# adaLN in the attention stages: from accumulations on VectorE to matrix products in quarters of TensorE's columns

## The chip, the cores and the metric

One core of one Trainium2 chip. The metric is the device time of one execution in microseconds (us), the median of several runs. TensorE (PE) multiplies; VectorE (DVE) and ScalarE (ACT) work elementwise; GpSimd (POOL) does little here; SyncE (SP) issues most of the DMA.

## What is computed

Two transformer blocks over 256 tokens of width 1024, in float32: a first block (gated recurrences, a long convolution, 32 experts of which each token uses two), then a second block of two layers (attention by retention and by a gated recurrence, then an MLP of width 4096). Every stage is modulated by adaLN: from a vector `c` come six vectors of 1024 (shift, scale and gate, twice), which are products of silu(c) with a 1024x6144 matrix.

```
def adaln(cvec, w, b):
    m = silu(cvec) @ w + b
    return split(m, 6)
...
mod_x = silu(c) @ ada_w[layer] + ada_b[layer]
mod_c = silu(c_ctx) @ ada_w[layer] + ada_b[layer]
...
hx = rmsnorm(x) * (1 + sc1) + sh1
```

In the second block's first layer both `c` and `c_ctx` need their vectors (two per matrix), in its second layer only `c` (one).

## The kernel before, in words

The kernel is written with a tile framework: the program's text gives instructions and priorities, and a scheduler decides at build time in which order each engine gets them, by its own estimate of times. Each engine then works through its list strictly in that order.

**Large products.** A weight tile of 1 MB is loaded into one of three `raw` buffers (`K.raw`, L175), split by ACT into a rounded part `whi` (L215) and by DVE into the rest `wlo` (L216), and multiplied in three products (`mm3`, L226 to L228). Their sums stand in PSUM: three buffers of the kind `mm`, two `tr`, three `at`.

**adaLN in two ways.** One adaLN vector set of 1024 columns is made in two **halves** of 512 columns, and a half needs two raw tiles of 512 x 512.
- `ada` (on DVE): for each of the 8 blocks of 128 rows and each vector, DVE scales the block by the vector's value in that row and adds it to `acc` (L287, L289). Then PE sums `acc` over the partitions, with one matrix product per 128 columns and vector that has a one in a single column (L296: 8 of them with two vectors, 4 with one), DVE copies (L299), PE transposes (L301), DVE copies (L302).
- `ada_pe` (on PE): 8 products per half with the two vectors as weights, 2 columns wide (L261), into an `mm` buffer; ACT copies the 2 rows (L265), PE transposes four times (L268).

A float32 product is two records in the trace, a transposition one.

**Where they run.** `ada_pe` makes one set at the program's start, one in the first block (`pieces`) and one ahead of the experts, from tiles that are already in memory (`adaw`). All others are `ada`: one at the start (two vectors), four in the first block (one vector), and in the second block three sets beside attention (gate, shift, scale; L1486) and one (layer 1) or three (layer 0) beside the MLP. They are generators in a list `s.bg`; `s.tick()` (called after a weight tile's load was written) runs one on to its next `yield`, which in `ada` comes after each raw tile.

**Attention** (block2). First the gated recurrence with four heads, one after the other, each a chain over all engines: PE transposes decayed keys (L1599), multiplies (L1613), DVE steps the state (L1628) and masks scores (L1637), PE makes the output (L1640, L1643). Beside it PE has the values `vr` (`values`, L1518 copies them from PSUM on ACT). Then retention, gates, output products.

Of the kernel before, what the change touches and what calls it, by code (L numbers as in the profile page):

```python
# [9 lines left out]
F32 = mybir.dt.float32  # L10
# [7 lines left out]
P = 128  # L18
# [8 lines left out]
def _consts():  # L27

    if CONSTS:
        return CONSTS  # L30
    f32, f64 = np.float32, np.float64
    p = np.arange(P)

    CONSTS["k_res"] = np.concatenate(
        [np.eye(P), np.tile((np.arange(24) == 15)[None], (P, 1)), np.tile(np.arange(8)[None], (P, 1))], 1).astype(f32)

# [86 lines left out]
class K:  # L123


    def __init__(self, nc, tc, I, out, cap=64, dbg=None):
# [12 lines left out]
        nc_ = nc  # L139
        self.kres = self.cp.tile([P, 160], F32, name="kres")  # L140
        nc_.scalar.dma_start(self.kres, I["k_res"])
        self.ident = self.kres[:, 0:128]
        self.hot = self.kres[:, 128:160]
        self.ones = self.cp.tile([P, 256], F32, name="ones")
# [100 lines left out]

    def ada_pe(self, pool, w, col0, s16, fin, got=()):

        nc = self.nc
        sv = s16.rearrange("p (i k) -> p k i", i=2)
        m = pool.tile([P, 16], F32, tag="adam", name="adam")  # L250
        for c in range(2):
            pt = self.mm()
            for q in range(2):
                if got:
                    v = got[c][:, 4 * q:4 * q + 4]
                else:
                    v = self.raw(w[512 * q:512 * q + 512, col0 + 512 * c:col0 + 512 * c + 512]
                                 .rearrange("(k p) c -> p k c", p=P))
                for kk in range(4):
                    k = 4 * q + kk  # L260
# [8 lines left out]
            nc.vector.tensor_copy(m.rearrange("p (i j) -> p j i", i=2)[:, 4 * c:4 * c + 4], p2[:, :, :2])  # L269
            yield  # L270
        fin(m)

    def ada(self, pool, w, col0, svecs, fin, tag="acc", src=()):
# [4 lines left out]
        for c in range(2):  # L278
            acc = pool.tile([P, nv, 512], F32, tag=tag, name="acc")
            for q in range(2):  # L280
# [10 lines left out]
                if q == 0:  # L291
                    yield
            n = 4 * nv
# [8 lines left out]
            nc.vector.tensor_copy(m.rearrange("p (i j) -> p i j", i=2)[:, :nv, 4 * c:4 * c + 4],  # L302
                                  p2[:, :n].rearrange("p (i j) -> p i j", j=4))
            if c == 1:
# [95 lines left out]
def params_c(s, pool):  # L400
# [7 lines left out]
    s.sc = s.cp.tile([P, 16], F32, name="sc")  # L408
    nc.scalar.activation(s.sc, pt[:, :16], AF.Silu)


# [15 lines left out]
def params(s, pool):  # L427
# [9 lines left out]
    s.sc2 = s.cp.tile([P, 16], F32, name="sc2")  # L437
    nc.scalar.activation(s.sc2, p1[:, 76:92], AF.Silu)
    s.cvw = p1[:, 0:36]
    s.n1g2 = [p1[:, 36 + 8 * l:44 + 8 * l] for l in range(2)]  # L440
# [92 lines left out]
def block1_mixer(s):  # L533
    nc, tc, I = s.nc, s.tc, s.I
    mt = nc.tensor.matmul
    with tc.tile_pool(name="p1", bufs=1) as pool_:
        pool = Pool(pool_, {"b8": 5, "b4": 3, "s4": 4, "t2": 6, "sq": 3,
                            "etot": 2, "adam": 2},
                    {"rstd": "s4", "nt": "sq", "prow": "sqo", "adarow": "sqo"})
        w_in = I["w_in"][0].rearrange("(k p) c -> p k c", p=P)  # L540
# [20 lines left out]

        both = [s.ada(pool, ada, 0, [sx, s.sc[:, 8:16]], fin0, "s4", (s.wp, "wlo")), s.ada_pe(pool, ada, 1024, s.sc, fin1)]
        for i in range(5):
# [79 lines left out]
        s.bg = [s.ada(pool, ada, 1024 * (i + 2), [sx], f) for i, f in enumerate((fin2, fin3, fin4, fin5))]  # L643
        pieces = s.ada_pe(pool, I["ada_w_2"][0], 0, s.sc2, fin0)

# [359 lines left out]
def moe(s):  # L1005
# [3 lines left out]
    with tc.tile_pool(name="pm", bufs=1) as pool_:  # L1009
        pool = Pool(pool_, {"xg": 2, "raw": 3, "sel": 2, "selT": 3, "hT": 2, "ws": 3, "glo": 3, "sq": 4},  # L1010
                    {"nt": "sq", "adarow2": "glo"})

        bias = s.adab2[0]

        def fin1(m):
            s.md2 += [fin_scale(s, m, 8 * i, bias[:, 8:16], s.n1g2[0], f"mA{i}") for i in range(2)]

        pieces = s.ada_pe(pool, I["ada_w_2"][0], 1024, s.sc2, fin1, s.adaw)
# [3 lines left out]
        tri, io64, io8 = km[:, 0:128], km[:, 128:256], s.kres[:, 152:160]  # L1022
        L = pool.tile([P, 2, 36], F32, name="L")
# [374 lines left out]
def block2(s):  # L1398
    nc, tc, I = s.nc, s.tc, s.I
    mt = nc.tensor.matmul  # L1400
    with tc.tile_pool(name="pb", bufs=1) as pool_:
        pool = Pool(pool_, {"b8": 5, "t2": 12, "nt": 3, "sx": 2, "rm": 1, "etot": 2, "st": 4},
                    {"sq": "t2", "acc": "b8"})
        kb = pool.tile([P, 2692], F32, name="kb2")
# [32 lines left out]
        def gla_params(l):  # L1437
# [9 lines left out]
            return gng, upst, gb  # L1447

        am = [pool.tile([P, 4, P], F32, name=f"am{i}") for i in range(2)]
        for a in am:  # L1450
            nc.gpsimd.memset(a, 0.0)

        for l in range(2):
# [508 lines left out]
```

## Time and profile before

| | us |
|---|---|
| three runs: median (lowest to highest) | 2025.29 (2024.18 to 2029.1) |
| the profiled execution | 2025.5 |
| its span in the trace | 2023.6 |
| TensorE busy in it | 1939.0 |
| VectorE busy | 1136.5 |
| ScalarE busy | 693.4 |

The span is the stretch from the first to the last instruction. PE's busy time counts overlapping records once; products overlap, and their ends are modelled, so that what one costs is read from the distance of starts. The stages: first block to 397 us, experts to about 890 us, second block's layer 0 with attention up to 1175 us and MLP up to 1540 us, layer 1 with attention up to 1790 us, then its MLP.

### The profile page before, as it was taken

Reading aid. Unit: us, or ns where it says so; the run is one execution under the profiler, and the core shown is the slowest. Engines: PE = TensorE matmul, PEld = TensorE weight load, DVE = VectorE, ACT = ScalarE, POOL = GpSimd, SP = SyncE. Lnnn points to the kernel's source line nnn. Section 1 sums busy time; section 2 is a strip of 40 time slices with the busy share of each in tenths; the row PEclk is TensorE's granted clock in tenths of the full one; section 3 lists DMA queues with packets and bytes.
Section 4 is the critical chain, followed back from the end, with each engine's and each line's share of the span. In section 5 each row is a group of like instructions: output and inputs, shape, how many; then the busy total and the mean of one; then the engine's idle time right before and its main releaser. Section 6 shows DMA issues by size and latency. Waiting matters only on the chain.

```text
span 2023.6 us, 27872 instructions
## 1 busy us (share of the span) xinstructions
PE 1939.0 (96%) x11492; PEld 1443.5 (71%) x11492; DVE 1136.5 (56%) x2110; ACT 693.4 (34%) x1023; POOL 32.2 (2%) x110
## 2 busy tenths in 40 slices
PE   6998989999999999989899999999999989999998
PEld 2866779844444444357678989778788967989998
DVE  5768795521101111144879959655634677887555
ACT  2564544421111111144432334131323454443444
POOL 0000000000000000000200000000000010000000
PEclk9999999999999999989989999999999989999999
DMA  8536546889999999953133424444423143457553
GB/s 285 167 105 208 167 130 231 309 364 421 421 421 421 420 421 421 421 205 104 43 125 126 149 82 135 157 146 135 135 84 104 56 148 114 156 197 229 175 180 104
DMA packets 218073, 426.15 MB, mean 211 GB/s; under 512 B 16427, under 2 KB 152584, under 8 KB 193112
## 3 DMA queue, kind: packets, MB, share of 16 engines
q1 hardware_dynamic: 208616, 419.75, 57.2%
q10 hardware_dynamic: 9200, 4.51, 0.8%
q8 instruction: 92, 1.51, 0.3%
q14 instruction: 37, 0.30, 0.0%
q0 software_dynamic: 128, 0.08, 0.0%
HBM read 423.26 MB, written 1.05 MB: 210 GB/s over the span
## 4 chain that ended last, share of the span: by engine, by line
PE 67%; DVE 6%; DMA 3%; ACT 2%; issue 1%; DVEq 0%; ACTq 0%; SPq 0%
PE mm L226 14%; PE mm L227 14%; PE mm L228 14%; PE mm L1271 10%; PE mm L1301 3%; PE at L1301 3%; DMA raw<-in_moe_w_down_dram 2%; PE at L1234 2%; PE at L1319 1%; PE tr L296 1%; DMA raw<-in_moe_w_up_dram 1%; DVE wlo L216 1%; DVE sx L1628 1%; DVE acc L289 1%; PE at L1712 1%
## 5 line engine op out<-in xcount | busy, mean ns | idle before, releaser
L228 PE MATMUL mm<-hh,wlo 128*128 128x256 f32 (+2 forms) x1232 | 406.3, 330 | 8.6 <-DVE wlo L216 8.6
L226 PE MATMUL mm<-hh,whi 128*128 128x256 f32 (+2 forms) x1232 | 411.4, 335 | 2.5 <-ACT hh L220 1.2
L227 PE MATMUL mm<-hl,whi 128*128 128x256 f32 (+2 forms) x1232 | 408.2, 332 | 0.1
L216 DVE TENSOR_TENSOR wlo<-raw,whi 128x2048 fp32r<-128x2048 f32 (+2 forms) x138 | 303.7, 2201 | 169.9 <-ACT whi L215 169.8
L215 ACT CAST whi<-raw 128x2048 fp32r<-128x2048 f32 (+2 forms) x138 | 253.1, 1834 | 354.0 <-PE mm L227 301.5
L228 PEld LDWEIGHTS mm<-hh,wlo 128*128 128x128 f32 (+1 forms) x1232 | 236.0, 192 | 33.3 <-DVE wlo L216 9.9
L226 PEld LDWEIGHTS mm<-hh,whi 128*128 128x128 f32 (+1 forms) x1232 | 236.2, 192 | 29.9 <-issue 3.8
L227 PEld LDWEIGHTS mm<-hl,whi 128*128 128x128 f32 (+1 forms) x1232 | 236.2, 192 | 25.7 <-issue 5.2
L289 DVE SCALAR_TENSOR_TENSOR acc<-raw,sc,acc 128x512 f32<-128x512 f32 x308 | 218.8, 746 | 13.9 <-DMA raw<-in_ada_w_dram 12.5
L226 PE MATMUL mm<-hidh,whi 128*128 128x256 f32 (+1 forms) x544 | 178.7, 331 | 0.0
L228 PE MATMUL mm<-hidh,wlo 128*128 128x256 f32 (+1 forms) x544 | 177.6, 330 | 0.1
L227 PE MATMUL mm<-hidl,whi 128*128 128x256 f32 (+1 forms) x544 | 177.3, 328 | 0.0
L1271 PE MATMUL mm<-raw,xg 128*64 128x512 f32 x736 | 172.5, 595 | 1.2 <-DMA raw<-in_moe_w_up_dram 1.2
L226 PE MATMUL mm<-whi,hh 128*128 128x256 f32 x512 | 150.1, 294 | 5.6 <-ACT vr L1518 3.6
L227 PE MATMUL mm<-wlo,hh 128*128 128x256 f32 x512 | 147.9, 289 | 3.0 <-DVE wlo L216 3.0
L228 PE MATMUL mm<-whi,hl 128*128 128x256 f32 x512 | 149.2, 292 | 0.7 <-DVE hl L371 0.7
L1271 PEld LDWEIGHTS mm<-raw,xg 128*64 128x64 f32 x736 | 54.6, 137 | 97.9 <-issue 93.2
L1279 DVE SCALAR_TENSOR_TENSOR glo<-mm,ws,glo 128x512 f32<-128x512 f32 x16 | 12.0, 751 | 191.1 <-PE mm L1271 169.2
L227 PEld LDWEIGHTS mm<-hidl,whi 128*128 128x128 f32 x544 | 102.3, 188 | 10.8 <-DVE hidl L221 0.6
L226 PEld LDWEIGHTS mm<-hidh,whi 128*128 128x128 f32 x544 | 101.9, 188 | 10.8 <-ACT hidh L220 0.7
L228 PEld LDWEIGHTS mm<-hidh,wlo 128*128 128x128 f32 x544 | 101.6, 188 | 11.0 <-DVE wlo L216 0.7
L226 PEld LDWEIGHTS mm<-whi,hh 128*128 128x128 f32 x512 | 99.6, 195 | 10.4 <-ACT vr L1518 4.8
(509 smaller groups left out, 2744.5 us busy)
## 6 DMA issues: line engine op xcount, KB each, us to landing
raw<-in_ada_w_dram SPq DMA_DIRECT2D x68, 1024.0 KB, 5.2
raw<-in_w_mlp_dram SPq DMA_DIRECT2D x64, 1024.0 KB, 5.4
raw<-in_w_in_dram SPq DMA_DIRECT2D x48, 1024.0 KB, 5.2
raw<-in_moe_w_down_dram SPq DMA_DIRECT2D x48, 1024.0 KB, 16.8
raw<-in_moe_w_gate_dram SPq DMA_DIRECT2D x46, 1024.0 KB, 13.9
raw<-in_moe_w_up_dram SPq DMA_DIRECT2D x46, 1024.0 KB, 15.6
rawh<-in_moe_w_gate_dram SPq DMA_DIRECT2D x18, 1024.0 KB, 13.2
rawh<-in_moe_w_up_dram SPq DMA_DIRECT2D x18, 1024.0 KB, 12.6
```

Of the source, the lines that this page charges most:

```text
L215: self.nc.scalar.copy(hv, v)
L216: self.nc.vector.tensor_tensor(lv, v, hv, op=OP.subtract)
L226: mt(out, ah, bh, start=first, stop=False)
L227: mt(out, ah, bl, start=False, stop=False)
L228: mt(out, al, bh, start=False, stop=last)
L289: nc.vector.scalar_tensor_tensor(acc[:, i], v[:, kk], s[:, k:k + 1], acc[:, i], op0=OP.mult, op1=OP.add)
L296: nc.tensor.matmul(pt[:n, :P], self.hot[:, 15 - r:15 - r + n], acc[:, r // 4, (r % 4) * P:(r % 4 + 1) * P], start=r == 0, stop=r == n - 1)
L1234: mt(px, tk[:, a, k * P:(k + 1) * P], sel[:, a], start=tk is th and a == 0, stop=tk is tl and a == 1)
L1271: mt(pg[64 * j:64 * j + 64], xg[:, k, 2 * i + j], vs[j][:, kk], start=k == 0, stop=k == 7)
L1301: mt(pd[c][sl], hT[:, k, sl], vs[j][:, kk, 512 * c:512 * c + 512], start=k == 0, stop=k == 3)
L1319: mt(po[:, j], y[:, i, sl], selT[:, i], start=y is yh and i == 0, stop=y is yl and i == 1)
L1628: nc.vector.scalar_tensor_tensor(sxs[ps_, b_], sxs[ps_, a_], etot[ps_, a_:a_ + 1], adds[a_][ps_], op0=OP.mult, op1=OP.add)
```

## The change

- `ada_pe` now has weights of 32 columns: the two vectors and 30 columns of zeros (`sw`, `sw2`). The four products of a raw tile go to four quarters of PE's columns and so to four groups of 32 PSUM rows, instead of one after the other into the same two rows. The copy takes 128 rows (L267 of the new file), and four products with a 0/1 matrix `pick2` add up the quarters and turn the result (L270).
- `ada` does the same with its partial sums: the products for the four 128-column pieces go to the four quarters (L300), and one product with `pick8` takes the place of the transposition (L305).
- The three sets beside attention in each of the two layers go from `ada` to `ada_pe`, with `rest=False`: there is one `yield` per half, so one tick asks for two raw tiles.
- In the second block the buffers of `nt` (3) and the copies `adarow`, `adarow2` go into the pool `t2`, which has 13 instead of 12; in the first block `adarow2` goes into `t2` with 6.

```diff
+    def ada_pe(self, pool, w, col0, s32, fin, got=(), rest=True):
...
-                    nc.tensor.matmul(pt[:2], sv[:, k], v[:, kk], start=k == 0, stop=k == 7)
-                if q == 0:
+                    nc.tensor.matmul(pt[32 * kk:32 * kk + 32], s32[:, 4 * q + kk], v[:, kk], start=q == 0, stop=q == 1)
+                if q == 0 and rest:
                     yield
-            row = pool.tile([2, 512], F32, name="adarow2")
-            nc.scalar.copy(row, pt[:2])
+            row = pool.tile([P, 512], F32, tag="adarow2", name="adarow2")
+            nc.scalar.copy(row, pt)
             p2 = self.tr((P, 4, 128))
             for j in range(4):
-                nc.tensor.transpose(p2[:, j, :2], row[:, j * P:(j + 1) * P], self.ident[:2, :2])
+                nc.tensor.matmul(p2[:, j, :2], row[:, j * P:(j + 1) * P], self.pick2, start=True, stop=True)
...
     def ada(self, pool, w, col0, svecs, fin, tag="acc", src=()):
...
-            for r in range(n):
-                nc.tensor.matmul(pt[:n, :P], self.hot[:, 15 - r:15 - r + n],
-                                 acc[:, r // 4, (r % 4) * P:(r % 4 + 1) * P], start=r == 0, stop=r == n - 1)
-            row = pool.tile([8, P], F32, tag="adarow", name="adarow")
-            nc.vector.tensor_copy(row[:n], pt[:n, :P])
+            for i in range(nv):
+                for j in range(4):
+                    nc.tensor.matmul(pt[32 * j:32 * j + 32, :P], self.hot[:, 31 - i:63 - i],
+                                     acc[:, i, j * P:(j + 1) * P], start=i == 0, stop=i == nv - 1)
+            row = pool.tile([P, P], F32, tag="adarow", name="adarow")
+            nc.vector.tensor_copy(row, pt[:, :P])
             p2 = self.tr()
-            nc.tensor.transpose(p2[:, :n], row[:n], self.ident[:n, :n])
+            nc.tensor.matmul(p2[:, :4 * nv], row, self.pick8[:, :4 * nv], start=True, stop=True)
...
-        pool = Pool(pool_, {"b8": 5, "t2": 12, "nt": 3, "sx": 2, "rm": 1, "etot": 2, "st": 4},
-                    {"sq": "t2", "acc": "b8"})
+        pool = Pool(pool_, {"b8": 5, "t2": 13, "sx": 2, "rm": 1, "etot": 2, "st": 4},
+                    {"sq": "t2", "acc": "b8", "nt": "t2", "adarow": "t2", "adarow2": "t2"})
...
-            s.bg = [s.ada(pool, ada, 1024 * i, vecs, fin(i)) for i in range(2, 5)]
+            s.bg = [s.ada_pe(pool, ada, 1024 * i, sw, fin(i), rest=False) for i in range(2, 5)]
```

What the build makes of it is seen in three lists.

**PE, layer 0, in the gated recurrence.** Before, around the first adaLN reduction (L296), in the last head; L226 to L228 are a large product, L1613 to L1643 a head's steps:

```order
2892 L1613 MATMUL at<-vm,ket 128x256 x4
2893 L1636 MATMUL at<-ec,cu 128x128 x4
2894 L296 MATMUL tr<-acc,kres 8x128 x4
2895 L228 MATMUL mm<-whi,hl 128x256
2896 L226 MATMUL mm<-hh,whi 128x512
2897 L227 MATMUL mm<-hl,whi 128x512
2898 L226 MATMUL mm<-hh,whi 128x512
2899 L227 MATMUL mm<-hl,whi 128x512
2900 L1636 MATMUL at<-ec,cu 128x128 x4
2901 L296 MATMUL tr<-acc,kres 8x128 x3
2902 L1640 MATMUL at<-vg,am_6355 128x128
2903 L1643 MATMUL at<-sx,ec 64x128 x2
```

With the change, the first adaLN products (L263), in the first head (L1628, L1651, L1655 and L1658 are L1613, L1636, L1640 and L1643 of before):

```order
2660 L1628 MATMUL at<-vm,ket 128x256 x4
2661 L1651 MATMUL at<-ec,cu 128x128 x4
2662 L230 MATMUL mm<-hl,whi 128x512
2663 L231 MATMUL mm<-hh,wlo 128x512
2664 L263 MATMUL mm<-raw,sw_6361 32x512 x5
2665 L1651 MATMUL at<-ec,cu 128x128 x4
2666 L263 MATMUL mm<-raw,sw_6361 32x512 x3
2667 L1655 MATMUL at<-vg,am_6364 128x128
2668 L1658 MATMUL at<-sx,ec 64x128 x2
```

Adaptive-norm work of this layer begins on PE three heads earlier than before, and the second four products are cut in two by a head's step.

**ACT, layer 0, the fourth head** (L1616 copies its turned keys, L1533 copies values, L267 copies adaLN sums from PSUM), with the change:

```order
432 L1607 ACTIVATE cu<-cu 128x512
433 L1608 ACTIVATE de<-de 128x512
434 L1533 COPY vr<-mm 128x256
435 L1616 COPY ket<-tr 128x512
436 L267 COPY adarow_7235<-mm 128x512
437 L267 COPY adarow_7262<-mm 128x512
438 L1704 ACTIVATE dc<-kb_6247,lg 128x2
439 L1705 ACTIVATE dc<-kb_6247,lg 128x2
440 L1533 COPY vr<-mm 128x256 x2
```

The sums of the first two halves, which PE makes in the first and second head, are copied here; until then they take two of the three `mm` buffers. Before, no such copy stood in ACT's list.

**SP, layer 0, attention.** Before:

```order
145 L175 DMA raw<-in_w_in_dram 128x8x256
146 L175 DMA raw<-in_ada_w_dram 128x4x512
147 L175 DMA raw<-in_w_in_dram 128x8x256
148 L175 DMA raw<-in_ada_w_dram 128x4x512
149 L175 DMA raw<-in_w_in_dram 128x8x256
```

With the change:

```order
146 L178 DMA raw<-in_w_in_dram 128x8x256
147 L178 DMA raw<-in_ada_w_dram 128x4x512 x2
148 L178 DMA raw<-in_w_in_dram 128x8x256
149 L178 DMA raw<-in_ada_w_dram 128x4x512 x2
150 L178 DMA raw<-in_w_in_dram 128x8x256
```

Two adaLN tiles now follow each weight tile, and they are let go by PE instead of DVE.

## Rows read from the trace of the kernel before

**Rows 1.** The page: busy time, share and instructions of each engine.
```profile
PE 1939.0 (96%) x11492; PEld 1443.5 (71%) x11492; DVE 1136.5 (56%) x2110; ACT 693.4 (34%) x1023; POOL 32.2 (2%) x110
```

**Rows 2.** Four stretches: length; PE, PEld, DVE, ACT, POOL busy; granted clock, DMA share, GB/s.
```profile
425.00:450.00 25.00, 25.00 (x144) 11.43 (x142) 2.37 (x11) 5.51 (x13) 0.00 (x0) 1.00 1.01 423
970.00:1032.00 62.00, 54.99 (x352) 42.72 (x348) 53.85 (x117) 23.27 (x47) 9.86 (x33) 0.91 0.19 59
1150.00:1165.00 15.00, 12.34 (x99) 11.71 (x99) 13.98 (x25) 5.12 (x6) 0.00 (x0) 0.99 0.56 186
1640.00:1695.00 55.00, 46.65 (x303) 37.93 (x302) 48.34 (x104) 28.25 (x60) 7.00 (x27) 0.91 0.30 97
```

**Rows 3.** Three of these stretches, adaLN accumulations (acc) alone: DVE busy, clock, DMA share, GB/s.
```profile
970.00:1032.00 62.00, 11.14 (x17) 0.91 0.19 59
1150.00:1165.00 15.00, 7.52 (x11) 0.99 0.56 186
1640.00:1695.00 55.00, 7.95 (x11) 0.91 0.30 97
```

**Rows 4.** Timeline of PE: start, length, line, operation; reductions, products of 2 and 64 rows.
```profile
28.34 1.91 PE L296 MATMUL tr<-acc,kres 128*8 128x128 f32 x16
30.08 1.02 PE L261 MATMUL mm<-raw,sc 128*2 128x512 f32 x2
...
119.00 1.04 PE L296 MATMUL tr<-acc,kres 128*4 128x128 f32 x8
...
127.42 3.60 PE L261 MATMUL mm<-raw,sc 128*2 128x512 f32 x8
...
419.91 3.64 PE L1271 MATMUL mm<-raw,xg 128*64 128x512 f32 x16
```

**Rows 5.** Timeline of PE: 16 records for quarters of the columns, and what follows.
```profile
149.37 0.66 PE L787 MATMUL po<-states,b 128*32 128x128 f32 x16
149.96 0.71 PE L783 MATMUL po<-vt,am 128*128 128x128 f32 x4
```

**Rows 6.** Timeline of PE: whole columns and halves of them in turn.
```profile
967.36 0.44 PE L1643 MATMUL at<-sx,ec 128*64 128x128 f32 x4
967.73 0.49 PE L1640 MATMUL at<-vg,am 128*128 128x128 f32 x2
968.15 0.44 PE L1643 MATMUL at<-sx,ec 128*64 128x128 f32 x4
```

**Rows 7.** Timeline of PE: 128x128 weights for one moving column.
```profile
1812.31 0.83 PE L341 MATMUL at<-ones,sq 128*128 128x1 f32 x6 [0.52 <-ACT sq L331]
```

**Rows 8.** Timeline of DVE, layer 0: accumulations ahead of other work.
```profile
1016.35 3.40 DVE L289 SCALAR_TENSOR_TENSOR acc<-raw,sc,acc 128x512 f32<-128x512 f32 x5
1019.67 5.27 DVE L1628 SCALAR_TENSOR_TENSOR sx<-sx,etot,at 64x128 f32<-64x128 f32 x14
...
1157.63 4.06 DVE L289 SCALAR_TENSOR_TENSOR acc<-raw,sc,acc 128x512 f32<-128x512 f32 x6
```

**Rows 9.** Timeline of PE, end of attention in layer 0 (idle before, releaser).
```profile
1162.95 0.66 PE L1757 MATMUL tr<-kres,orr 128*128 128x128 f32 x4 [1.67 <-DVE hl L221]
```

**Rows 10.** Timeline of PE: a product that waits for a PSUM copy.
```profile
992.99 0.39 PE L226 MATMUL mm<-whi,hh 128*128 128x256 f32 x1 [0.93 <-ACT vr L1518]
```

**Rows 11.** Timelines at the start of the experts: PE, then the DMA queue.
```profile
409.87 4.46 PE L261 MATMUL mm<-adaw,sc 128*2 128x512 f32 x10
...
414.36 1.71 SPq L1148 DMA_DIRECT2D rawh<-in_moe_w_gate_dram  x2
```

**Rows 12.** Timeline of PE at the program's start.
```profile
48.57 0.40 PE L268 MATMUL tr<-kres,adarow 2*128 2x2 f32 x4 [0.67 <-ACT adarow L265]
...
55.10 0.38 PE L226 MATMUL at<-whi,hh 128*128 128x256 f32 x1 [3.23 <-ACT hh L370]
```

More of the change, by code (lines that the diff above doesn't have):

```diff
@@ L34, in _consts @@
     CONSTS["k_res"] = np.concatenate(
-        [np.eye(P), np.tile((np.arange(24) == 15)[None], (P, 1)), np.tile(np.arange(8)[None], (P, 1))], 1).astype(f32)
+        [np.eye(P), np.tile((np.arange(64) == 31)[None], (P, 1)), np.tile(np.arange(8)[None], (P, 1)),
+         p[:, None] == 32 * (np.arange(8) % 4)[None] + (np.arange(8) // 4)[None],
+         p[:, None] % 32 == np.arange(2)[None]], 1).astype(f32)
     r = np.repeat(np.arange(T // 64, dtype=f32), 64)
@@ L139, in __init__ @@
         nc_ = nc
-        self.kres = self.cp.tile([P, 160], F32, name="kres")
+        self.kres = self.cp.tile([P, 210], F32, name="kres")
         nc_.scalar.dma_start(self.kres, I["k_res"])
         self.ident = self.kres[:, 0:128]
-        self.hot = self.kres[:, 128:160]
+        self.hot = self.kres[:, 128:192]
+        self.pick8, self.pick2 = self.kres[:, 200:208], self.kres[:, 208:210]
         self.ones = self.cp.tile([P, 256], F32, name="ones")
@@ L243, in param_pack @@
         nc.vector.tensor_copy(self.par[:, i], pt[:, :P])
-    def ada_pe(self, pool, w, col0, s16, fin, got=()):
+    def ada_pe(self, pool, w, col0, s32, fin, got=(), rest=True):
         nc = self.nc
-        sv = s16.rearrange("p (i k) -> p k i", i=2)
         m = pool.tile([P, 16], F32, tag="adam", name="adam")
@@ L409, in params_c @@
     nc.scalar.activation(s.sc, pt[:, :16], AF.Silu)
+    s.sw = pool.tile([P, 8, 32], F32, name="sw")
+    nc.vector.memset(s.sw, 0.0)
+    nc.vector.tensor_copy(s.sw[:, :, 0:2], s.sc.rearrange("p (i k) -> p k i", i=2))
 def params0(s, pool):
@@ L438, in params @@
     nc.scalar.activation(s.sc2, p1[:, 76:92], AF.Silu)
+    s.sw2 = s.sw
+    nc.vector.tensor_copy(s.sw2[:, :, 0:2], s.sc2.rearrange("p (i k) -> p k i", i=2))
     s.cvw = p1[:, 0:36]
@@ L538, in block1_mixer @@
                             "etot": 2, "adam": 2},
-                    {"rstd": "s4", "nt": "sq", "prow": "sqo", "adarow": "sqo"})
+                    {"rstd": "s4", "nt": "sq", "prow": "sqo", "adarow": "sqo", "adarow2": "t2"})
         w_in = I["w_in"][0].rearrange("(k p) c -> p k c", p=P)
@@ L560, in fin1 @@
             md["Ac"] = fin_scale(s, m, 8, s.adab[:, 8:16], s.n1g, "mAc")
-        both = [s.ada(pool, ada, 0, [sx, s.sc[:, 8:16]], fin0, "s4", (s.wp, "wlo")), s.ada_pe(pool, ada, 1024, s.sc, fin1)]
+        both = [s.ada(pool, ada, 0, [sx, s.sc[:, 8:16]], fin0, "s4", (s.wp, "wlo")), s.ada_pe(pool, ada, 1024, s.sw, fin1)]
         for i in range(5):
@@ L643, in block1_mixer @@
         s.bg = [s.ada(pool, ada, 1024 * (i + 2), [sx], f) for i, f in enumerate((fin2, fin3, fin4, fin5))]
-        pieces = s.ada_pe(pool, I["ada_w_2"][0], 0, s.sc2, fin0)
+        pieces = s.ada_pe(pool, I["ada_w_2"][0], 0, s.sw2, fin0)
         def proj(c0, n, act=None):
@@ L1013, in moe @@
         bias = s.adab2[0]
+        s.sw2 = pool.tile([P, 8, 32], F32, name="sw2")
+        nc.vector.memset(s.sw2, 0.0)
+        nc.vector.tensor_copy(s.sw2[:, :, 0:2], s.sc2.rearrange("p (i k) -> p k i", i=2))
         def fin1(m):
             s.md2 += [fin_scale(s, m, 8 * i, bias[:, 8:16], s.n1g2[0], f"mA{i}") for i in range(2)]
-        pieces = s.ada_pe(pool, I["ada_w_2"][0], 1024, s.sc2, fin1, s.adaw)
+        pieces = s.ada_pe(pool, I["ada_w_2"][0], 1024, s.sw2, fin1, s.adaw)
         cols = s.cols
@@ L1021, in moe @@
         nc.scalar.dma_start(km, I["k_moe"])
-        tri, io64, io8 = km[:, 0:128], km[:, 128:256], s.kres[:, 152:160]
+        tri, io64, io8 = km[:, 0:128], km[:, 128:256], s.kres[:, 192:200]
         L = pool.tile([P, 2, 36], F32, name="L")
@@ L1447, in gla_params @@
             return gng, upst, gb
+        sw = pool.tile([P, 8, 32], F32, name="sw2")
+        nc.gpsimd.memset(sw, 0.0)
+        nc.gpsimd.tensor_copy(sw[:, :, 0:2], s.sc2.rearrange("p (i k) -> p k i", i=2))
         am = [pool.tile([P, 4, P], F32, name=f"am{i}") for i in range(2)]
```

7 lines of the change are left out of this document (3 added, 4 removed).

## The prediction

> **What bounds the kernel.** I read the page first. PE is busy for 1939.0 of 2023.6 us [rows 1], so as a rule one microsecond of PE work more or less is one of time. Then the busy time of each engine by stretches of 25 or 50 us, to find where that rule fails. It fails in three kinds of place. Among the experts PE is busy too, but the DMA share is 1.01 at 423 GB/s [rows 2]: transfers set that stage. In the gated recurrences of both layers DVE is busy for 53.85 of 62 and 48.34 of 55 us while PE stands still for 7.0 and 8.35 us, at a mean granted clock of 0.91, that is with part of the stretch at 1.2 instead of 2.4 GHz [rows 2]. At the end of layer 0's attention DVE has 13.98 of 15 us [rows 2]. So beside attention there are stretches where DVE leads, and the adaLN accumulations take 11.14, 7.52 and 7.95 us of DVE in them [rows 3]. The timelines show how: five accumulations run from 1016.35 and the state step of the last head begins only at 1019.67, with no gap [rows 8]; six run from 1157.63, and PE then waits 1.67 us for DVE's `hl` [rows 8, 9].
>
> The change takes work off DVE where DVE leads, puts it on PE, and makes all adaLN work on PE cheaper if quarters of its columns run at once. All three have to be priced.
>
> **What one half (512 columns) costs on PE.** A float32 product of 512 columns is two records; eight of them take 3.60 us, two 1.02, so a record starts every (3.60-1.02)/6 = 0.43 us when products follow each other [rows 4]. On halves of the columns, in the experts, 16 records take 3.64 us, 0.2 us each: two at a time [rows 4]. Quarters exist once in the trace: 16 records of 128 columns begin at 149.37 and the next operation at 149.96, 0.59 us [rows 5], where 16 one after the other take 1.74 us (28.34 to 30.08) [rows 4]. That is three times as fast with the run-out of the last ones in it, and four chains of four would take 0.44. For 512 columns the run-out weighs less, so I take four at a time: 16 x 0.43 / 4 = 1.7 us per half. The bounds are 2.3 (three times) and 3.4 us (pairs).
>
> The Trainium skill ("TensorE: Matmul & The Clock Gate", measured speedup in the part on row and column tiling) gives 2.38 for three column tiles, 0.79 of the ideal. Four at 0.79 would make 2.15 us of the 1.7, an estimate, and the sum below 6 us longer.
>
> Going to another width and back: halves and whole columns in turn take 0.37 us for four records and 0.42 for two [rows 6]; two whole ones alone are 0.22 by the 0.11 above, so a change of width costs some 0.2 us, 0.4 per half. New are four products with 128x128 weights and two moving columns, eight records; six of the like take 0.83 us [rows 7], so 1.1 us. A half is thus 1.7 + 0.4 + 1.1 = 3.2 us.
>
> **The change, part by part.**
> - Layer 0, six halves moved. Removed from PE: 1.74 us for 16 records and 0.14 for a transposition (one record, priced by rows 7), 1.9 us. Added 3.2, so 6 x 1.3 = 7.8. In the order of the change two groups of four are cut by a head's step; the lone product then runs without partners, 0.86 us each, 1.7. Sum **+9.5**.
> - Layer 1, six halves with one vector: removed 0.87 + 0.14 = 1.0 each, so 6 x 2.2 = 13.2, and three cuts, 2.6: **+15.8**.
> - The set on PE in the first block, two halves: 16 x 0.43 and 0.40 for the turns [rows 12] are 7.3, now 3.2, with two cuts: -6.5. Part lies in a recurrence of that block whose chain sets the pace, so I take **-4**.
> - Reductions that stay on DVE's side: six halves with two vectors beside layer 0's MLP go from 1.74 to 0.59 + 0.4 for the widths + 0.14 for a second record of the turn: **-3.7**. The ten with one vector (eight records) go from 0.87 to 0.3 + 0.4 + 0.14, nothing.
> - Program start: PE waits for tiles there, but behind the last tile it has products one after another, and the first large product waits 3.23 us for ACT and the modulation [rows 12]. Between 0 and -4, **-2**.
> - Experts: the DMA queue asks for the next expert tile at 414.36, just as the ten last adaLN records end (409.87 + 4.46) [rows 11]. Those tiles take over the adaLN tiles' memory. The new order has these products done before the router's; then the router's own result is next in line a little earlier. Since DMA sets the stage, what is saved at its head stays saved: 0 to -4.46, **-2**. DVE has a memset and a small copy more here, a few tenths, in the same chain.
> - DVE beside attention loses 26.6 us in the three stretches [rows 3]. Not all of it delays somebody (some accumulations run while DVE would wait), and what is late next is the chain's own steps on ACT and PE. Above nothing and below 26.6 I take four fifths, as DVE's share there is 0.87 to 0.93 [rows 2], 21, and 2 more for a clock that falls less often (0.09 of 117 us is 10.5 us of clock lost): **-23**. That also holds the place of the first adaLN products, which stand in gaps of the recurrence.
> - ACT gets 12 copies of 128 x 512 from PSUM, DVE loses the small ones; ACT is busy a third of the time [rows 1], so I take nothing for that. SP's order becomes weights, adaLN, adaLN; with a DMA share of 0.19 to 0.56 in these stretches [rows 2] two tiles in a row are hidden, unless PE is late in freeing them. Zeroing the padded weights is POOL's or lies ahead of the first tiles. Other buffers of `nt` and of the copies: nothing, since DVE no longer holds `acc` there.
>
> Sum: 9.5 + 15.8 - 4 - 3.7 - 2 - 2 - 23 = -9.4. The profiled execution took 2025.5 us, against a median of 2025.29, so the two agree to 0.2 and the sum needs no correction: **2016 us**.
>
> **The rivals.**
> 1. *Three times instead of four.* If 512 columns overlap no better than the short ones [rows 5], a half is 0.6 us dearer, on the 14 halves that lie on PE's path: +8, **2024 us**. The Trainium skill's 0.79 for three tiles (above) lies close to this. For it: the only row with quarters. Against it: that row has the run-out in it.
> 2. *Pairs.* If the two records of one product hold up the next product, four quarters run two at a time, as the halves do [rows 4]: 1.7 us more on 14 halves and some 2 in the reductions, **2042 us**, slower. It decides as soon as a half's products take over 2.6 us: then the moved work costs PE more than DVE's relief returns. Against it: 16 records in 0.59 us can't be pairs, which would take 0.87 [rows 5].
> 3. *Sums that are not fetched.* ACT copies the first two halves' sums only after the fourth head's keys, so two of three `mm` buffers are held over nearly the whole recurrence and the values' products run through the one that is left. Before, PE waited 0.93 us where such a copy came late [rows 10]. Five such waits in layer 0 and three in layer 1 are 7 us, and PE has less to fill gaps with, so half of the 23 is lost: 2016 + 7 + 11.5 = **2034.5 us**, slower. For it: the lists. Against it: the heads' own steps stand between several of these products.
> 4. *All of it comes back.* The 26.6 us and 5 of the clock return instead of 23, and two halves in layer 0 fill gaps at no cost (6): **2002 us**. For it: DVE's shares. Against it: ACT's steps are in the same chain.
>
> **The numbers.** Forecast 0.46, with 8 us either way from the unknown prices; rivals 0.15, 0.10, 0.14 and 0.15 in their order. The range runs from rival 4 to rival 3, **2001 to 2035**; it leaves out the pairs and tails of the others. A difference of 0.3% (6 us) is about what a measurement can tell, so faster is below 2019.2 and slower above 2031.4. Faster: 0.7 of the forecast, all of rival 4, a little of rival 1: 0.49. Slower: rival 2, two thirds of rival 3, tails: 0.22. The same: 0.29.
>
> **What would show it.** Right: 16 records of L263 starting within some 1.9 us; in the two recurrences DVE less busy by 11 and 8 us with a higher granted clock, and the stretch to the end of layer 0's attention shorter by some 5 us, layer 1's about as long as before; the layer 0 MLP shorter by some 4. Wrong: L263 records 0.2 us apart (rival 2); PE waiting for ACT's copies of `vr` or L263 for a DMA (rival 3); DVE freed but the heads at the same distance, so that the chain was never DVE's.

## The result and the profile after

The change makes the kernel **slower**: 2047.84 us (median of 4 runs, 2042.17 to 2051.24) against 2024.88 us of the kernel before on the same chip, a ratio of 1.0107 (95% interval 1.0089 to 1.0126). The prediction said 2016 us, at most 2035. The profiled execution took 2048.05 us, its span is 2046.3.

The page, as [rows 1]:

```profile
PE 1928.7 (94%) x11666; PEld 1445.7 (71%) x11666; DVE 1047.3 (51%) x1959; ACT 702.0 (34%) x1037; POOL 29.8 (1%) x112
```

PE has 10 us less to do and DVE 89, and the span is 22.7 longer: PE stands still more, 117.6 instead of 84.6 us. To see where, I cut both spans at the same six instructions: the last L973 (before the experts), the last L1319 (their end), the last L1757 of layer 0 and of layer 1 (end of attention) and the last product of layer 0's MLP (lines of the kernel before). Layer 0's MLP ends at 1593 us by these cuts, not at the 1540 given with the stages of before. The lengths between them, in us; "forecast" is the prediction's sum with the 23 us of DVE's relief shared out as the accumulations are in [rows 3], 18.66 to 7.95:

| stage | before | change | difference | forecast |
|---|---|---|---|---|
| start and first block | 396.9 | 399.2 | +2.3 | -6 |
| experts | 491.9 | 495.1 | +3.2 | -2 |
| layer 0, attention | 283.8 | 286.4 | +2.6 | -6.6 |
| layer 0, MLP | 420.4 | 414.5 | -5.9 | -3.7 |
| layer 1, attention | 194.1 | 214.3 | +20.2 | +8.9 |
| layer 1, MLP | 236.6 | 237.0 | +0.4 | 0 |

Layer 1's attention alone is nearly the whole loss. The stretches that answer to [rows 2], and three parts of layer 1's recurrence (length; PE, PEld, DVE, ACT, POOL busy; granted clock, DMA share, GB/s):

```profile
976.00:1038.00 62.00, 57.83 (x378) 45.84 (x378) 45.53 (x115) 25.49 (x48) 8.03 (x33) 0.92 0.19 62
1155.00:1172.00 17.00, 14.87 (x124) 14.39 (x123) 8.90 (x19) 6.60 (x9) 0.00 (x0) 1.00 0.19 63
1645.00:1705.00 60.00, 48.57 (x284) 32.02 (x282) 42.67 (x105) 27.02 (x60) 6.18 (x24) 0.80 0.32 106
1650.00:1664.00 14.00, 8.57 (x35) 4.51 (x36) 9.92 (x21) 5.71 (x10) 1.89 (x8) 0.66 0.69 232
1664.00:1680.00 16.00, 12.48 (x50) 6.10 (x51) 9.84 (x28) 8.54 (x19) 0.20 (x1) 0.55 0.22 63
```

DVE is relieved as foreseen: its share falls from 0.87 to 0.73 in layer 0's recurrence and from 0.88 to 0.71 in layer 1's. Layer 0's recurrence became shorter: from the first head's last output product to the fourth's it takes 57.3 instead of 61.5 us. Layer 1's hardly did: from its first L1572 to its last L1643 (L1587 and L1658 with the change) it takes 60.0 instead of 61.0. In layer 1, between 1650 and 1680, PE is idle for 9 of 30 us and its mean granted clock is 0.66 and 0.55, close to the lower level of 1.2 GHz; in the same two stretches of before it was 0.76 and 1.00. PE's timeline there (start, length, line, operation, idle before and releaser):

```profile
1650.10 0.44 PE L1587 MATMUL tr<-kres,e 128*128 128x128 f32 x2 [0.61 <-DVE e L1584]
1650.46 1.06 PE L263 MATMUL mm<-raw,sw 128*32 128x512 f32 x6
...
1657.01 1.23 PE L1651 MATMUL at<-ec,cu 64*128 64x128 f32 x8
1662.42 0.79 PE L1655 MATMUL at<-vg,am 128*128 128x128 f32 x2 [4.18 <-DVE am L1652]
1663.15 0.70 PE L1658 MATMUL at<-sx,ec 128*64 128x128 f32 x4
...
1675.26 1.23 PE L1651 MATMUL at<-ec,cu 64*128 64x128 f32 x8
1676.42 2.83 PE L263 MATMUL mm<-raw,sw 128*32 128x512 f32 x16
1679.19 0.39 PE L229 MATMUL mm<-whi,hh 128*128 128x256 f32 x1
```

Through two heads there is not one large product: the first of the values' products begins at 1679.19. Before, some 100 records of them stood in these heads. PE waits 4.18 us where it had waited 2.36:

```profile
1655.93 0.55 PE L1640 MATMUL at<-vg,am 128*128 128x128 f32 x2 [2.36 <-DVE am L1637]
```

The longer wait alone is no mark of the change: e4 and e5 below have values' products in these heads and wait 3.41 and 4.10 us there. The heads' own steps take longer at the lower clock (four records of L1658 in 0.70, in 0.44 at the full one). Still the recurrence as a whole is no longer than before. What it lost is what ran beside the heads: 109 records of large products instead of 205. The others run behind it, where the stage takes 99.2 instead of 80.5 us from the recurrence's end.

ACT's list suggests why no buffer was free:

```profile
1671.63 2.35 ACT L1550 COPY kst<-mm 64x512 f32<-64x512 f32 x4
1674.01 1.55 ACT L1554 ACTIVATE qst<-mm 64x256 f32<-64x256 f32 x4
...
1701.47 1.08 ACT L267 COPY adarow<-mm 128x512 f32<-128x512 f32 x2
```

The rows leave out the buffers' numbers. By this order two of the three `mm` buffers hold the next heads' keys and queries until they are copied from 1671.63 and 1674.01 on, and the third, in which the values' products ran before, holds the adaLN sums of the first half until 1701.47. That is the mechanism of the prediction's third rival; e2 measures what it costs in each layer.

**The price on PE came out as priced.** In the stretch behind the recurrence, at full clock:

```profile
1720.45 1.92 PE L263 MATMUL mm<-raw,sw 128*32 128x512 f32 x16
1722.30 0.50 PE L229 MATMUL mm<-hh,whi 128*128 128x512 f32 x1
...
1723.33 0.95 PE L270 MATMUL tr<-kres,adarow 128*128 128x2 f32 x8
1724.14 0.48 PE L230 MATMUL mm<-hl,whi 128*128 128x512 f32 x1
```

16 records in quarters take 1.85 us with the change of width in it, against 16 x 0.43 = 6.9 one after the other: 3.7 times as fast. The eight small ones take 0.81. Over layer 1's attention the distances from an adaLN record to the next start add up to 19.4 us for six halves, 3.2 each (the prediction's figure; some of them ran at the lower clock), against 5.7 before: +13.7, where +13.2 and 2.6 for cuts were taken.

A reduction of two vectors is cheaper than foreseen. In the MLP its eight records of one vector take 0.36 us (two rows here are one half's two vectors):

```profile
1256.65 0.43 PE L300 MATMUL tr<-acc,kres 128*32 128x128 f32 x8
1257.01 0.50 PE L229 MATMUL mm<-hh,whi 128*128 128x512 f32 x1
...
1257.90 0.43 PE L300 MATMUL tr<-acc,kres 128*32 128x128 f32 x8
```

adaLN's time on PE in that MLP falls from 14.0 to 4.5 us; 3.3 of the 9.5 are lost again at its beginning to two new waits for DVE (0.90 and 2.43 us).

**The first block and the experts.** In the first block the slow products had kept PE busy until 136.25, while ACT made the rounded part `whi` of the next weight tile. Now they are done early, but ACT makes `whi` later, and PE waits for it. PE with the change, then before:

```profile
127.06 1.06 PE L263 MATMUL mm<-raw,sw 128*32 128x512 f32 x8
128.05 1.16 PE L728 MATMUL at<-vt,kt 128*128 128x128 f32 x8
134.77 0.58 PE L229 MATMUL mm<-hh,whi 128*128 128x256 f32 x1 [5.56 <-ACT whi L218]
...
178.75 0.39 PE L305 MATMUL tr<-kres,adarow 128*128 128x4 f32 x2 [2.33 <-DVE adarow L303]
181.21 0.65 PE L300 MATMUL tr<-acc,kres 128*32 128x128 f32 x8 [2.08 <-DVE acc L292]
```

```profile
136.25 0.39 PE L226 MATMUL mm<-hh,whi 128*128 128x256 f32 x1
```

ACT with the change, then before:

```profile
131.42 1.28 ACT L742 ACT_TABLE_LOAD   x1
...
132.83 1.88 ACT L218 CAST whi<-raw 128x2048 fp32r<-128x2048 f32 x1
```

```profile
130.18 1.88 ACT L215 CAST whi<-raw 128x2048 fp32r<-128x2048 f32 x1
```

In this stretch ACT stands still neither before nor now. In its list three table loads (1.28 us each, from 127.77, 129.29 and 131.42) now stand just ahead of `whi` where one stood, so that `whi` is ready at 134.7 instead of 132.1. The large product that begins at 134.77 began at 136.25 before: 6 us of cheaper products gave 1.5, and reductions that come earlier in PE's list then wait for DVE.

At the entry to the experts the products that had run, as ten slow records, while the routing was worked out [rows 11] are done before it now, and PE stands still for its result. PE with the change, then before:

```profile
411.24 0.63 PE L1102 MATMUL at<-sele,ones 128*128 128x32 f32 x4 [2.95 <-DVE sele L1095]
...
416.77 0.58 PE L1246 MATMUL at<-sel,th 128*128 128x256 f32 x1 [3.82 <-DVE sel L1232]
417.36 0.63 PE L1246 MATMUL at<-sel,tl 128*128 128x256 f32 x2
```

```profile
414.79 0.40 PE L1234 MATMUL at<-sel,tl 128*128 128x256 f32 x2
```

Counted from the stage's beginning, the routing's result comes only 0.4 us later than before. But after these waits the granted clock is 0.62 from 416.7 to 424 us, where it was 1.00 before, and the 24 records from L1246's first on (L1234 before) take 5.3 instead of 3.25 us. That makes 2 of the stage's 3.2 us; the rest was not followed. The next expert tile is asked for at 414.36, as before [rows 11].

### The profile page after: what moved, and what is told of

Same layout as the page of the kernel before. It is cut to its first block, busy times and chain, and to the rows that moved or that the text cites. A ratio compares the mean times of both kernels' runs of the same rounds, so it can differ in the third digit from the quotient of the medians.

```text
span 2046.3 us, 28094 instructions
## 1 busy us (share of the span) xinstructions
PE 1928.7 (94%) x11666; PEld 1445.7 (71%) x11666; DVE 1047.3 (51%) x1959; ACT 702.0 (34%) x1037; POOL 29.8 (1%) x112
## 4 chain that ended last, share of the span: by engine, by line
PE 66%; DVE 6%; DMA 5%; ACT 2%; issue 1%; DVEq 0%; ACTq 0%; SPq 0%
PE mm L229 14%; PE mm L231 13%; PE mm L230 13%; PE mm L1283 9%; PE mm L1313 3%; PE at L1313 3%; DMA raw<-in_moe_w_down_dram 2%; PE at L1246 2%; PE at L1331 1%; DVE wlo L219 1%; DMA raw<-in_moe_w_up_dram 1%; PE mm L263 1%; ACT whi L218 1%; DMA rawh<-in_moe_w_gate_dram 1%; PE at L1628 1%
## 5 line engine op out<-in xcount | busy, mean ns | idle before, releaser
L231 PEld LDWEIGHTS mm<-hh,wlo 128*128 128x128 f32 (+1 forms) x1232 | 236.9, 192 | 38.4 <-DVE wlo L219 15.3
L292 DVE SCALAR_TENSOR_TENSOR acc<-raw,sc,acc 128x512 f32<-128x512 f32 x182 | 129.3, 746 | 10.4 <-DMA raw<-in_ada_w_dram 9.5
L231 PEld LDWEIGHTS mm<-hidh,wlo 128*128 128x128 f32 x544 | 102.0, 189 | 11.2 <-DVE wlo L219 1.0
## 6 DMA issues: line engine op xcount, KB each, us to landing
raw<-in_moe_w_up_dram SPq DMA_DIRECT2D x46, 1024.0 KB, 14.6
rawh<-in_moe_w_up_dram SPq DMA_DIRECT2D x18, 1024.0 KB, 11.3
```

The source lines that it names most:

```text
L231: mt(out, al, bh, start=False, stop=last)
L292: nc.vector.scalar_tensor_tensor(acc[:, i], v[:, kk], s[:, k:k + 1], acc[:, i], op0=OP.mult, op1=OP.add)
```

## The experiments

Theories when they were made. **Held**: adaLN sums keep the `mm` buffer that the values' products need. **Queue**: two adaLN tiles in a row bring the values' weight tiles late. **Relief**: what DVE gives back is worth less than 23 us.

**e1: layer 1 on DVE again.**

```diff
-            s.bg = [s.ada_pe(pool, ada, 1024 * i, sw, fin(i), rest=False) for i in range(2, 5)]
+            s.bg = [s.ada_pe(pool, ada, 1024 * i, sw, fin(i), rest=False) if l == 0
+                    else s.ada(pool, ada, 1024 * i, vecs, fin(i)) for i in range(2, 5)]
```

> The change, but layer 1's three sets beside attention are accumulated on DVE again (with the new reductions). By the comparison of the two traces layer 1's attention took 20.4 us more than before, all of it between the start of its gated recurrence and the products after it. If the moved work of that layer is the cause, this kernel takes 2047.8 - 20.4 = about 2027 us (2023 to 2031). If the loss came from something that the whole kernel has (the wider copies, the shared buffers), it stays above 2038 us.

Measured: 2026.06 us, ratio to before 0.9999 (0.9988 to 1.0010). Layer 1's attention takes 192.4 us. The loss is that layer's moved work; its cheaper reductions (2.8 instead of 5.7 us of PE) are a small gain.

**e2: a buffer of its own for the copies.**

```diff
-        pool = Pool(pool_, {"b8": 5, "t2": 13, "sx": 2, "rm": 1, "etot": 2, "st": 4},
-                    {"sq": "t2", "acc": "b8", "nt": "t2", "adarow": "t2", "adarow2": "t2"})
+        pool = Pool(pool_, {"b8": 5, "t2": 12, "sx": 2, "rm": 1, "etot": 2, "st": 4, "adarow2": 1},
+                    {"sq": "t2", "acc": "b8", "nt": "t2", "adarow": "t2"})
```

> The change, but the copies of the adaLN sums have one buffer of their own in the second block and the shared pool has 12 instead of 13, the same memory. ACT's list then has the copy of the first half's sums in the first head of each recurrence instead of after the fourth head's keys, so one mm buffer more is free from there on. Theory 'held' (two mm buffers keep adaLN sums, two keep the next heads' keys and queries until 1671.63 and 1674.01, so the values' products have no buffer in the first two heads of layer 1, PE stands still and the clock falls): 5 to 14 us return, 2034 to 2043 us. Theory 'queue' (the values' weight tiles are asked for 14 us later, behind two adaLN tiles): no change, 2045 to 2051 us.

Measured: 2036.37 us, 1.0051 (1.0035 to 1.0067). 11.5 us return, in the range of "held". But the stages say otherwise than I had thought: layer 0's attention falls from 286.4 to 278.9 us, layer 1's only from 214.3 to 210.4. Holding the sums cost 7.5 us in layer 0 and 3.9 in layer 1, and layer 1's loss is mostly another.

**e3: one tile at a time.** (`rest=False` taken out.)

> The change, but with a stop after each adaLN tile, so that one tile at a time stands between the values' weight tiles, as before. Theory 'queue': most of layer 1's 20 us return, 2029 to 2036 us. Theory 'held': PE's list still has no values' product in the first two heads of layer 1 and the sums are still held, so little changes, 2042 to 2050 us.

Measured: 2041.78 us, 1.0077 (1.0052 to 1.0103), just under the range of "held" and far from that of "queue". Layer 0 gains 6.8 us (279.6), layer 1 none to speak of (213.3).

**e4: what DVE's relief is worth.** In the kernel before:

```diff
-                for kk in range(4):
+                for kk in range(1 if thin else 4):
```

> The kernel before, in which the sets beside attention accumulate only 2 of 8 row blocks (the other products are left out): all loads, reductions and waits stay, DVE loses three quarters of these accumulations. It measures what DVE's relief beside attention is worth by itself. The prediction took 23 us for all of it, which makes some 17 us here: 2008 us. Rival: the accumulations stood mostly in gaps that DVE has anyway between the steps of the chain, and the relief is worth 5 us or less: 2020 to 2025 us.

Measured: 2018.63 us, 0.9959 (0.9946 to 0.9971): 7.6 us, not 17. By stage 8.4 of it lie in layer 0's attention (275.4), and layer 1's is as long as before (194.7 against 194.1), although three quarters of that layer's accumulations are gone too. The heads of layer 1 (first L1572 to the fourth head's) take 46.6 us with the thin accumulations and took 45.7: that recurrence gained nothing from a freer DVE.

In layer 0 most of the gain has one place, the last head and the ten microseconds behind it. The third head's output products begin 0.6 us earlier than before (at 1008.17 before), the last head's 2.3 (at 1027.13); the 521st record of a large product in this stage begins 8.8 us earlier, at 1029.33 instead of 1038.08. PE in the kernel before, last head:

```profile
1022.81 1.13 PE L1636 MATMUL at<-ec,cu 64*128 64x128 f32 x8
1026.38 0.82 PE L296 MATMUL tr<-acc,kres 128*8 128x128 f32 x6 [2.45 <-DVE acc L289]
1027.13 0.49 PE L1640 MATMUL at<-vg,am 128*128 128x128 f32 x2
...
1030.42 0.80 PE L1640 MATMUL at<-vg,am 128*128 128x128 f32 x2
```

and in e4:

```profile
1020.59 1.16 PE L1636 MATMUL at<-ec,cu 64*128 64x128 f32 x8
...
1024.80 0.38 PE L1640 MATMUL at<-vg,am 128*128 128x128 f32 x2
...
1027.05 0.49 PE L1640 MATMUL at<-vg,am 128*128 128x128 f32 x2
```

Before, a reduction (L296) stands in PE's list ahead of the head's output products (L1640) and waits 2.45 us for an accumulation. Then the clock falls (0.80 instead of 0.49 for the same two records): from 1030 to 1040 us the granted clock is 0.58 before and 1.00 in e4. In layer 1 no reduction waits like that.

The reduction is not the only thing that kept PE there. DVE in the kernel before:

```profile
1024.97 0.72 DVE L1637 COPY_PREDICATED am<-kb,at 128x512 f32<-128x512 int32 x1
1025.59 0.74 DVE L289 SCALAR_TENSOR_TENSOR acc<-raw,sc,acc 128x512 f32<-128x512 f32 x1
1026.24 0.72 DVE L1637 COPY_PREDICATED am<-kb,at 128x512 f32<-128x512 int32 x1
```

The output products need both masks `am`, and the second is ready only at 1026.96, after the accumulation: without the reduction PE would have waited for it. In e4 the second mask is ready at 1024.14, and 13 records of large products stand in PE's list where before there was the reduction alone. Which of these the gain needs was not separated. e9 below keeps the accumulations and has such a wait too (2.44 us, at 1032.84).

**e5: the sums in another kind of PSUM buffer.** On top of e2:

```diff
-            pt = self.mm()
+            pt = self.mm() if rest else self.at()
```

> e2_row_buffer, and the adaLN sums of the sets beside attention stand in a PSUM buffer of the kind at instead of mm. PE's list then has the values' products in the first two heads of both recurrences again, as before the change, and the adaLN products at their end. Theory 'held' (what layer 1 loses beyond the price of the products on PE is the third mm buffer): layer 1 loses only the price, six halves of 2.66 us (1.85 for 16 records with the change of width, 0.81 for the eight small ones) less 1.2 removed, some 9 us instead of 20; with e2's 9 us in layer 0 that is 2028 us (2024 to 2032). Theory 'queue': the values' weights still come behind two adaLN tiles, layer 1 stays as in e2, 2036 us.

Measured: 2054.68 us, 1.0141 (1.0118 to 1.0164). Both theories miss. The values' products are back in the first two heads of both layers, and layer 1 still takes 214.0 us, layer 0 even 294.4 (why is open). The heads' own products use the `at` buffers, so that this is not a clean test of the `mm` buffers alone. In layer 1 waits have come behind the recurrence:

```profile
1721.74 1.07 PE L263 MATMUL at<-raw,sw 128*32 128x512 f32 x8 [1.84 <-DMA raw<-in_ada_w_dram]
1723.57 1.87 PE L270 MATMUL tr<-kres,adarow 128*128 128x2 f32 x8 [0.76 <-ACT adarow L267]
1726.66 0.79 PE L229 MATMUL mm<-hh,whi 128*128 128x512 f32 x1 [1.22 <-ACT whi L218]
```

**e6: layer 1's halves behind the recurrence.** (No `tick` while the values' tiles are asked for there.)

> The change, but in layer 1 no adaLN tile is asked for while the values' weight tiles are, so all six halves run behind the recurrence, where PE has no gaps. It measures the price on PE alone: 6 x (2.66 - 1.2) = 9 us in layer 1 instead of 20.4, 2036 us (2033 to 2040). If the products cost more than that beside large products, or if the loss was never in the recurrence, over 2042 us.

Measured: 2049.30 us, 1.0108 (1.0082 to 1.0133); layer 1's attention 212.9 us, and layer 0's, which the edit does not touch, 289.9, 3.5 more than in the change. Missed: the price is not 9 us. I had worked it out from one half's rows at full clock and had taken 1.2 us off per half for the reductions, where the rows before add up to 5.7 for six. Here too PE waits once more for weights, at the gates:

```profile
1793.03 0.39 PE L230 MATMUL mm<-wlo,hh 128*128 128x256 f32 x1 [2.81 <-DVE wlo L219]
```

Layer 1's attention of five kernels, PE's time by the distance from each record's start to the next, idle time taken out; then the length of its recurrence (us) and the large products' records in it:

| | length | large products | adaLN | other | idle | recurrence | large in it |
|---|---|---|---|---|---|---|---|
| before | 194.1 | 135.9 | 5.7 | 42.6 | 9.9 | 61.0 | 205 |
| e4, thin accumulations | 194.7 | 133.7 | 5.8 | 44.0 | 11.2 | 59.0 | 195 |
| change | 214.3 | 133.8 | 19.4 | 48.6 | 12.4 | 60.0 | 109 |
| e5, sums in `at` | 214.0 | 138.4 | 18.2 | 42.7 | 14.7 | 57.1 | 181 |
| e6, late | 212.9 | 135.6 | 19.2 | 44.3 | 13.8 | 59.2 | 193 |

Wherever the six halves stand, they cost 12.5 to 13.7 us of PE, and some 5 to 7 of waits and lower clock come on top: in the first two heads (change, in "other" and idle), behind the recurrence (e5), or at the gates (e6). The recurrence itself takes 57 to 61 us in all five; what a kernel does not fit into it runs behind it.

**e7: e1 and e2 together.**

> e1 and e2 together: layer 1 on DVE, layer 0 on PE with a buffer of its own for the copies. If the two effects are independent: 2026.1 - 9 = 2017 us (2013 to 2021). If e2's gain in layer 0 needs something else, 2026.

Measured: 2016.28 us, 0.9951 (0.9937 to 0.9966). The two effects add up; layer 0's attention takes 279.1 us.

**e8: the first block and the experts as before.** (Their adaLN set has products two columns wide again, the first block's reductions the old form.)

> e7, and the first block's adaLN set and reductions and the experts' set go back to the form of before (only the program's start keeps quarters there). In the traces of the change and of e1 to e3 the second block begins 6 to 10 us later than before. If the quarters of the first block and the experts' entry make that, it returns: e7 less 6 to 10, some 2009 us (2006 to 2013). If it is only how such runs vary, the same as e7.

Measured: 2013.82 us, 0.9940 (0.9917 to 0.9963). 2.5 us return, less than expected, and little more than the runs of one kernel differ (2014.97 to 2018.38 in e7). By stage the first block is at 397.3 and the experts at 492.3 (e7: 398.1 and 494.4; change: 399.2 and 495.1). The experts' entry is most of it; the program's start gains 2.5 us by 105 us in this run and has lost them by 180.

**e9: cheaper reductions alone.** (The kernel before with L300 and L305 in the second block.)

> The kernel before with one part of the change alone: the second block's reductions in quarters (12 halves with two vectors in layer 0, 6 with one in layer 1); nothing is moved from DVE, everything ahead of the second block is as before. By the change's trace six such halves beside layer 0's MLP went from 14.0 to 4.5 us of PE time, of which 3.3 were lost to waits that a pool of the change made. So 9.5 in the MLP, some 6 in layer 0's attention (10.5 us of reductions there), 1.7 in layer 1 (e1): 2025.5 - 17 = 2008 us (2005 to 2013). If the reductions beside attention stand in gaps of PE, only 11 of it: 2014 us. If the gain in layer 0 needs the move, e8's 2013.8 stays the better one by 5 or more.

Measured: 2013.46 us, 0.9929 (0.9908 to 0.9950). Layer 0's attention gains 6.5 us (277.3), its MLP 7.0 (413.4), layer 1's attention 1.9 (192.2), as worked out. In the profiled execution, the slowest of the four at 2016.28, the first block is 6.3 us longer (403.2), though only the buffer of one small copy and a wider tile of constants differ there; why was not tried. Without that it would be about 2007, an estimate. So the cheaper reductions alone, with nothing moved, bring as much as e8, which also moves layer 0's three sets.

**e10: e8, one tile at a time.**

> e8 with a stop after each adaLN tile in layer 0. e3 gained 6 us in layer 0 by this without the buffer of its own. Theory 'held': with the buffer the order of tiles no longer matters, 2012 to 2016 us, as e8. Theory 'queue' as a second, independent loss: 4 to 6 us less, 2008 to 2010 us.

Measured: 2010.25 us, 0.9915 (0.9894 to 0.9936), 3.6 us under e8 and just over the range of "queue": layer 0's attention 273.6 instead of 278.9, its MLP 2.2 longer. So the order of tiles is a loss of its own in layer 0, beside the held buffers.

**e11: only the first of layer 0's sets moved.**

```diff
-            s.bg = [s.ada_pe(pool, ada, 1024 * i, sw, fin(i), rest=False) if l == 0
+            s.bg = [s.ada_pe(pool, ada, 1024 * i, sw, fin(i), rest=False) if l == 0 and i == 2
```

> e8 with only the first of layer 0's three sets on PE, the other two on DVE with the reductions in quarters. The first set runs in the recurrence, where e4 says that DVE's relief is worth 9 us; the other two stand beside retention and gates, where e4's gain does not grow (8.9 us at 1060, 8.8 at 1150), and cost PE some 1.3 us per half. Expected 4 to 5 us less than e8: 2009 us (2006 to 2013). If the relief at the end of the attention stage counts too (DVE led there for 14 of 15 us), 2014 to 2018 us.

Measured: **2002.74 us**, 0.9880 (0.9860 to 0.9900), better than expected and the best of all. Layer 0's attention takes 269.2 us: adaLN costs PE 9.7 us there (10.5 before, 18.3 in the change), and the last head's wait is gone. Its recurrence and layer 1's, columns as above:

```profile
960.00:1023.00 63.00, 59.74 (x422) 45.52 (x422) 58.43 (x132) 26.21 (x49) 13.20 (x47) 1.00 0.31 102
1634.00:1690.00 56.00, 51.43 (x338) 41.77 (x339) 47.79 (x114) 25.86 (x58) 4.40 (x19) 0.94 0.33 107
```

DVE is busy for 0.93 of layer 0's recurrence, more than before [rows 2], and PE runs through it at full clock. Why it is better than expected the rows show in part: the set's products stand ahead of the second head's steps, where PE had waited 2.88 us for DVE. Before, then e11:

```profile
973.04 0.66 PE L1599 MATMUL tr<-kres,de 128*128 128x128 f32 x4 [2.88 <-DVE de L1594]
```

```profile
969.78 1.06 PE L263 MATMUL mm<-raw,sw 128*32 128x512 f32 x8
971.11 1.06 PE L263 MATMUL mm<-raw,sw 128*32 128x512 f32 x8 [0.27 <-DMA raw<-in_ada_w_dram]
972.73 0.66 PE L1653 MATMUL tr<-kres,de 128*128 128x128 f32 x4 [0.55 <-DVE de L1648]
```

From 970 to 980 us the granted clock was 0.68 and is 1.00. By the split used for layer 1, layer 0's attention gains 3.9 us in large products (176.3), 6.5 in other products (67.8), 3.4 in idle time (15.3) and 0.8 in adaLN: mostly the same products in less time, at a higher clock.

**e12: e11, one tile at a time.**

> e11 with the stop of e10 after each adaLN tile: in layer 0's recurrence the second half comes behind values' products. If e10's 5 us in layer 0's recurrence (the values' products begin in the second head instead of behind its steps) add to e11: 1997 us (1994 to 2001). If e11 has them already, since only one set's two halves stand there: 2001 to 2004 us.

Measured: 2003.66 us, 0.9889 (0.9873 to 0.9906): no difference from e11 that could be told. Layer 0's attention is 2.7 us shorter (266.5), the MLP behind it 4.7 longer (419.2).

**e13: one set in layer 1 too.**

> e11 with the first set moved in layer 1 too: two of six halves, which run in its recurrence. e4 says that DVE's relief is worth nothing in layer 1. Theory 'price': two halves of 3.2 us less 0.5 of reductions that are in quarters there, 5.5 us, and the third mm buffer that they hold costs waits and clock in the first two heads, some 3 to 6 more: 2008 to 2014 us. Theory 'relief' (DVE sets the pace of layer 1's recurrence too, and the change lost it only by moving all three sets): 2002 us or less.

Measured: 2007.96 us, 0.9911 (0.9894 to 0.9927), 5.2 more than e11; in the profiled execution layer 1's attention is 2.4 longer, with 5.8 more of adaLN on PE. "Relief" falls: even two halves that stand in or ahead of the recurrence cost time. How much is less sure: 5.2 us by the medians, about their price, but 2.4 in the stage of the profiled execution, which was the fastest of the four (2004.47).

## Why the prediction was wrong

- **The step that failed is DVE's relief, -23 us.** I took four fifths of 26.6 us because DVE was busy for 0.87 to 0.93 of those stretches. Of the 16.1 us that fall on layer 0 the change got 5.2 (adaLN costs PE 7.8 more, the stage is 2.6 longer), and of layer 1's 6.9 nothing. e4 measures 7.6 for three quarters of the accumulations, all in layer 0 and mostly in one head, around a wait of 2.45 us that stood in the trace of before at 1026.38; I had quoted only DVE's side of that head [rows 8]. The busy share did not say which work delays somebody: e11's DVE is busier in layer 0's recurrence than before, and that layer's attention is 14.6 us shorter (269.2), against 4.7 in e7 (279.1), which relieves DVE of all three sets. The two other sets cost PE 8.5 us there and gave nothing back.
- **Held buffers were priced at nothing.** Rival 3 saw the mechanism and took 18.5 us for it, five waits in layer 0 to three in layer 1 and half of the relief. e2 gets back 11.5 in all, 7.5 in layer 0 and 3.9 in layer 1.
- **Layer 1: +15.8 on PE was nearly right (13.7), -6.9 of relief was not there, and 6.5 came on top.** The heads' own steps lost their cover and ran at the lower clock, and the products that had run beside them ran behind the recurrence. Giving the copies a buffer (e2) gets back no more than 3.9 of layer 1's 20 us.
- **Layer 0: +9.5 on PE was 7.8** (18.3 - 10.5). With the sums held the relief did not cover it, with a buffer of its own for the copies it did: e2 is 4.9 us shorter than before in that stage.
- **First block, -4, and start, -2.** The start gained 2.4 us (instructions at 105 us). The -4 was the cover read wrongly: I took the slow products for what kept PE, but PE goes on with a weight tile that ACT has rounded, and in ACT's new order that comes 2.65 us later.
- **Experts, -2:** +3.2. I had the order of PE and SP in view, but not that the slow products had filled PE's wait for the routing: uncovered, it is followed by a lower clock, and the products behind it take 2 us more.
- **Reductions in the MLP, -3.7:** -9.5 of PE time, -5.9 with two new waits. Eight records of one vector take 0.36 us, and a half takes 0.76 in all instead of the 1.27 of the prediction; before it had taken 2.33 rather than 1.88.
- **Four at a time was right** against rivals 1 and 2: 3.7 times over 16 records. The Trainium skill's 2.38 for three column tiles ("TensorE: Matmul & The Clock Gate", measured speedup in the part on row and column tiling) is 0.79 of three; this case's rows with four give 0.93 of four, and the rows decide.

The errors by stage, 8.3 + 5.2 + 9.2 - 2.2 + 11.3 + 0.4, make the 32 us between forecast and result.

## What to carry to other kernels

A busy share says how much an engine does, not whom it delays. Before work is moved off an engine, find a row in which another engine waits for just that work, as the 2.45 us here; thinning that work in the old kernel (e4) measures what relief alone brings. Look also where the moved work will stand: in a gap of its new engine, as the 2.88 us of e11, it can bring more than the relief. And ask which buffers it will hold, and what ran in them: cheaper products cost more than their price when they take the place of the work that filled another chain's gaps. Here the cheaper reductions alone brought 0.7% (e9), with one set of six moved 1.2% (e11); with all six moved the kernel lost 1.1%.

## What stays open, and what was unexpected

Why some 5 to 7 us of waits come with layer 1's six halves wherever they stand is not settled. That two of the three weight buffers are taken by adaLN tiles at a time may be a part, but no run shows it: e3, which asks for one at a time, shortens that layer by 1 us only; both remedies together were not tried there. Every edit also lets the scheduler order all lists anew, so that stages change which the edit does not touch, as layer 0 in e6 and the first block in e9. What a single part is worth is known here only to some microseconds.

What I had not expected of the chip: products in quarters of the columns lose almost nothing to each other (1.85 us for what takes 6.9 in turn), and the clock's two levels make a short wait dear. In the stretch with the 4.18 us wait and the one behind it (granted clock 0.66 and 0.55) PE is near 1.2 GHz, and 16 such quarter records take 2.77 us (1676.42 to 1679.19) instead of 1.85.
